# The gate of an RWKV-7 layer: computed per unit of the recurrence, or for half the sequence at a time and kept in DRAM

## The chip, the cores and the metric

The kernel runs on one core of a Trainium2 chip. The metric is device time in microseconds, one launch, median of the runs shown. Engines: PE (TensorE, matrix products), DVE (VectorE), ACT (ScalarE), POOL (GpSimd) and SP (SyncE, which here only issues DMAs). Each engine works through its instructions in the order in which they were written for it, and waits at an instruction until its operands are there.

## The reference, cut to what matters

One sequence of 1024 tokens, width 1024, float32. Two layers: an RWKV-7 time mixing with an MLP, then an attention layer with an MLP. The change lies in the RWKV-7 layer:

```
xg = h + (token_shift(h) - h) * mu[5]
g = sigmoid(xg @ g1) @ g2              # g1: 1024 x 160, g2: 160 x 1024, g: 1024 x 1024
...                                    # r, w, k, v, a in like manner; wkv7_scan gives y
y = groupnorm(y) * ln_w + ln_b + bonus
x = x + (1 + gt1) * ((y * g) @ wo)
x = x + (1 + gt2) * mlp(...)           # 1024 -> 4096 -> 1024, squared ReLU
```

The sigmoid's 160 outputs per token are the LoRA values. The gate g is their product with g2.

## The kernel before, in words

Activations lie with 128 channels on the partitions and tokens along the row: a matrix of 1024 channels is 8 tiles (`KT`), a half of the sequence is 512 tokens (`HT`).

**Large products.** `mm3` makes a product of float32 accuracy from three fp32r products: both operands are split into a high part (rounded to fp32r) and a low part (the rest), and high by high (line 124), low activation by high weight (126) and high activation by low weight (128) are summed. `load_w` fetches a weight tile of 128 x 1024 into `wraw` (115), ACT rounds it to `wh` (116), POOL subtracts to get `wl` (117). `wraw`, `wh` and `wl` have two buffers each (`NW = (2, 2)`), which every stream of weights shares. `proj` walks over 8 output tiles with one such weight each: 24 products for one half, 48 where both halves share a weight. It is a generator, and yields after each of the 8 steps.

**Small products** (the scan's, the LoRA's, the norm's) take float32 operands as they are; such a product appears as two PE instructions in the trace.

**The recurrence** runs in 16 units (`units`): 8 pairs of channel tiles by four quarters of 256 tokens, in this order: first half of the sequence for all pairs, then the second. Each unit has an `early` and a `late` part, which prepare it, a serial `chain` with priority, and afterwards a `gate`, run beside the next unit. At each stop of the chain, `step` takes so many steps of the others: `NA` (2.2 in units 0 to 6), `NC` and `NB` for the stream beside. That stream (`m0`, from `beside` in `run`) first finishes the projections (`dense`: v for the first half, then the second half's `lora_wa`, k, v, r streams and `lora_g`), waits until the first half's gates are done, and then goes on with the output projection `wo` and the MLP of the first half. After the units come 20 more steps of it (`ND`), then `wo` for the second half, and so on; `m1` is the second half's MLP. Later `phase_kv` makes the keys, values and forget gate logits that both halves of the attention layer use, with `proj` over both halves and the weights of K and V in turn; the forget gate's own weight (128 x 8 x 16) stands among them.

**The gate before.** `lora_g` makes the LoRA values for a half. 128 of them go to DRAM (`gad`), the last 32 to partitions 96 to 127 of `zt` in SBUF. `gate` norms the unit's y, fetches `ga` (128 x 256) and for each of two channel tiles a piece of g2, makes the gate with two float32 products (943, 944) into PSUM, and DVE multiplies (946):

```
PE.matmul(out=ps[:, c], lhsT=g2[:, 0], rhs=ga, start=True, stop=False)
PE.matmul(out=ps[:, c], lhsT=g2[96:128, 1], rhs=self.zt[96:128, ts], start=False, stop=True)
...
V.tensor_tensor(out=y, in0=y, in1=ps, op=ALU.mult)
```

**Who sets the order.** The code is written as one program; when it is built, a scheduler lays each engine's instructions in an order by its own estimate of times, within the dependences and priorities. A change in one place therefore reorders others, also far behind it.

Of the kernel before, what the change touches and what calls it, by code (L numbers as in the profile page):

```python
# [15 lines left out]
F32 = mybir.dt.float32  # L16
F32R = mybir.dt.float32r
BF16 = mybir.dt.bfloat16
AF = mybir.ActivationFunctionType
ALU = mybir.AluOpType  # L20
# [3 lines left out]
T = 1024  # L24
HT = 512
D = 1024
KT = 8
# [48 lines left out]
class K:  # L76
# [171 lines left out]
    def run(self, stop=99):  # L248
        tc, nc, ap = self.tc, self.nc, self.ap
        V, S = nc.vector, nc.scalar  # L250
        with ExitStack() as es:
# [45 lines left out]
            self.T16d = dt("T16d", [2 * KT, 2, 64, 256])  # L297
            self.gad = dt("gad", [128, T])

# [9 lines left out]
            zp = self.pool(er, "zp")  # L309
            self.zt = zp.tile([128, T], F32, name="zt")  # L310
            self.sv = zp.tile([128, KT, HD], F32, name="sv")
# [109 lines left out]
    NS = 1.5  # L421
    NA = 2.2
    NW = (2, 2)
# [22 lines left out]
    def phase_rwkv(self, es):  # L446
# [85 lines left out]

        def dense():
            yield from v
            yield from self.lora_wa(h, 1, lw, al)
            for i in (1, 2, 0):
                yield from self.stream(h, 1, i, xj, ev, al)
            yield from self.lora_g(h, 1, lw)

# [30 lines left out]
    def lora_g(self, h, j, lw):  # L570

        nc, S = self.nc, self.nc.scalar
        s = slice(j * HT, (j + 1) * HT)
        ps = [self.bank() for _ in range(2)]
        for k in range(KT):
            w = lw(("g1",), k)
            xg = self.mix(h[j][k], self.shift(h[j][k]), 5, k)
            for p, o, n in ((ps[0], 0, 128), (ps[1][96:128], 128, 32)):
                nc.tensor.matmul(out=p, lhsT=w[:, o:o + n], rhs=xg, start=k == 0, stop=k == KT - 1)
                yield  # L580
        g = self.t()
        for a, p in ((g, ps[0]), (self.zt[96:128, s], ps[1][96:128])):
            S.activation(out=a, in_=p, func=AF.Tanh, scale=0.5)
            nc.gpsimd.tensor_scalar(out=a, in0=a, scalar1=0.5, scalar2=0.5, op0=ALU.mult, op1=ALU.add)
        nc.sync.dma_start(out=self.gad[:, s], in_=g)

# [86 lines left out]
    def phase_wkv(self, es, rest, done):  # L673
# [18 lines left out]
        def lng(n, shape, bufs=2):  # L692
            return pool["s"].tile(shape, F32, name=n, tag=n, bufs=bufs)
# [228 lines left out]
        def gate(u, w):  # L922

            j, p, ts = where(u)
            y, bv, rs = w["y"], self.t(), self.t()
            ga = lng("ga", [128, 256], 1)
            nc.sync.dma_start(out=ga, in_=self.gad[:, ts])
            nc.sync.dma_start(out=two(bv), in_=pair(self.bvd, p, ts))
# [5 lines left out]
            S.activation(out=rs, in_=rs, func=AF.Exp, scale=-0.5)  # L934
            ps = self.small()
            for q in range(2):
                c = slice(q * 256, (q + 1) * 256)
                g2 = lng("g2", [128, 2, 128], 1)
                nc.sync.dma_start(out=g2[:, 0], in_=ap["g2"][p + q][0:128])
                nc.sync.dma_start(out=g2[96:128, 1], in_=ap["g2"][p + q][128:160])  # L940
                V.scalar_tensor_tensor(out=y[:, c], in0=y[:, c], scalar=self.col("lnw", p + q), in1=rs[:, c], op0=ALU.mult, op1=ALU.mult)
                V.scalar_tensor_tensor(out=y[:, c], in0=y[:, c], scalar=self.col("lnb", p + q), in1=bv[:, c], op0=ALU.add, op1=ALU.add)
                PE.matmul(out=ps[:, c], lhsT=g2[:, 0], rhs=ga, start=True, stop=False)
                PE.matmul(out=ps[:, c], lhsT=g2[96:128, 1], rhs=self.zt[96:128, ts], start=False, stop=True)
                yield
            V.tensor_tensor(out=y, in0=y, in1=ps, op=ALU.mult)
            nc.sync.dma_start(out=pair(self.yd, p, ts), in_=two(y))
# [522 lines left out]
```

## Time and profile before

| | |
|---|---|
| median of 3 runs | 3394.84 us (3390.83 to 3399.28) |
| the profiled execution | 3394.05 us, its span 3392.1 us |
| PE busy | 3214.4 us (95%) |
| DVE, ACT, POOL busy | 1943.0 (57%), 1432.8 (42%), 1358.7 (40%) |
| mean granted TensorE clock | 0.970 |

The span is the time from the first to the last instruction. A busy time is the time in which an engine works on some instruction; PE's products overlap, so a product's place in the row is best read as the distance from its start to the next one's start. The granted clock has two levels, full speed (2.4 GHz) and half of it (1.2 GHz); a figure between is a mean over a stretch. The units lie between about 243 and 1320 us.

### The profile page before, as it was taken

What the parts mean: (1) busy time and instruction counts of PE and PEld (TensorE: products, weight loads), DVE (VectorE), ACT (ScalarE), POOL (GpSimd) and SP (SyncE); (2) the same over time, 40 slices, a digit from 0 to 9 for tenths busy, and PEclk for the clock granted to TensorE, in tenths of its full rate; (3) what the DMA queues carried; (4) which work ended last, traced back from release to release, by engine and by line L of the source; (5) the groups of instructions that cost most, each with busy time, mean ns of one, the idle gap of its engine ahead of it and who ended that gap; (6) DMA issues with size and microseconds to landing.
All of it is one profiled execution on the core that took longest, in us unless ns stands there. A gap on an engine that the chain in (4) does not pass through costs nothing.

```text
span 3392.1 us, 50350 instructions
## 1 busy us (share of the span) xinstructions
PE 3214.4 (95%) x19108; PEld 2438.4 (72%) x19108; DVE 1943.0 (57%) x3239; ACT 1432.8 (42%) x2284; POOL 1358.7 (40%) x868
## 2 busy tenths in 40 slices
PE   4898999999999999899999999999999999999997
PEld 2456666666777776678887777777778888778886
DVE  7496765766556534167786433555566666454344
ACT  3642236523433223242233556667555544332323
POOL 3364432333333233354444432444423333454444
PEclk7899999899999999899999999999999999999999
DMA  7374344355333223236752233666544443232222
GB/s 276 98 234 151 95 128 135 116 152 150 88 102 102 85 76 125 68 111 224 229 187 88 85 131 119 207 203 182 177 128 136 144 134 100 88 111 95 98 98 83
DMA packets 294065, 452.90 MB, mean 134 GB/s; under 512 B 114720, under 2 KB 170432, under 8 KB 293824
## 3 DMA queue, kind: packets, MB, share of 16 engines
q1 hardware_dynamic: 293824, 449.68, 42.3%
q8 instruction: 152, 2.49, 0.3%
q14 instruction: 89, 0.73, 0.1%
HBM read 371.25 MB, written 78.32 MB: 133 GB/s over the span
## 4 chain that ended last, share of the span: by engine, by line
PE 50%; DVE 4%; ACT 2%; DMA 1%; issue 1%; POOL 1%; SPq 0%; DVEq 0%; ACTq 0%; POOLq 0%
PE pj L124 8%; PE pj L128 7%; PE pj L126 7%; PE pk L128 7%; PE pk L124 7%; PE pk L126 7%; PE pt L1328 2%; PE po L1313 1%; PE po L1314 1%; PE ps L1285 1%; PE ps L1286 1%; DVE t L239 1%; DVE hl L241 1%; DVE x L1016 1%; DVE modacc L185 0%
## 5 line engine op out<-in xcount | busy, mean ns | idle before, releaser
L117 POOL TENSOR_TENSOR wl<-wraw,wh 128x1024 fp32r<-128x1024 f32 x385 | 947.7, 2462 | 1231.7 <-ACT wh L116 1162.6
L116 ACT CAST wh<-wraw 128x1024 fp32r<-128x1024 f32 x385 | 402.6, 1046 | 822.0 <-PE pk L126 359.2
L124 PE MATMUL pj<-hh,wh 128*128 128x512 f32 x1120 | 448.6, 408 | 7.4 <-DVE sq L1090 2.7
L128 PE MATMUL pj<-hh,wl 128*128 128x512 f32 x1120 | 445.1, 403 | 5.5 <-POOL wl L117 5.5
L126 PE MATMUL pj<-hl,wh 128*128 128x512 f32 x1120 | 443.2, 401 | 0.0
L1016 DVE SCALAR_TENSOR_TENSOR x<-pj,G,x 128x512 f32<-128x512 f32 x304 | 225.8, 747 | 164.3 <-PE pj L128 162.2
L128 PE MATMUL pk<-hh,wl 128*128 128x512 f32 x688 | 272.1, 402 | 8.6 <-POOL wl L117 8.6
L124 PE MATMUL pk<-hh,wh 128*128 128x512 f32 x688 | 270.2, 398 | 8.9 <-ACT wh L116 7.8
L126 PE MATMUL pk<-hl,wh 128*128 128x512 f32 x688 | 267.3, 395 | 0.0
L124 PEld LDWEIGHTS pj<-hh,wh 128*128 128x128 f32 x1120 | 210.9, 189 | 61.9 <-issue 4.5
L1016 DVE SCALAR_TENSOR_TENSOR x<-pk,G,x 128x512 f32<-128x512 f32 x240 | 176.2, 746 | 135.7 <-PE pk L128 135.2
L128 PEld LDWEIGHTS pj<-hh,wl 128*128 128x128 f32 x1120 | 210.6, 188 | 58.9 <-POOL wl L117 7.7
L126 PEld LDWEIGHTS pj<-hl,wh 128*128 128x128 f32 x1120 | 211.1, 189 | 48.1 <-issue 2.4
L124 PE MATMUL pj<-mh,wh 128*128 128x512 f32 x564 | 236.9, 421 | 6.0 <-DVE mr L1046 3.0
L126 PE MATMUL pj<-ml,wh 128*128 128x512 f32 x564 | 224.3, 398 | 0.0
L128 PE MATMUL pj<-mh,wl 128*128 128x512 f32 x564 | 219.4, 399 | 2.4 <-POOL wl L117 2.4
L124 PE MATMUL pk<-mh,wh 128*128 128x512 f32 x460 | 182.1, 398 | 8.9 <-DVE mr L1046 5.4
L166 ACT CAST mh<-mr 128x512 fp32r<-128x512 f32 x128 | 79.5, 621 | 250.6 <-PE pj L128 109.1
L126 PE MATMUL pk<-ml,wh 128*128 128x512 f32 x460 | 181.7, 395 | 0.0
L185 DVE SCALAR_TENSOR_TENSOR modacc<-modw,cact,modacc 128x1024 f32<-128x1024 f32 x98 | 155.1, 1583 | 31.0 <-DMA modw<-in_modw_dram 22.5
L128 PE MATMUL pk<-mh,wl 128*128 128x512 f32 x460 | 166.6, 397 | 0.0
L124 PEld LDWEIGHTS pk<-hh,wh 128*128 128x128 f32 x688 | 130.7, 190 | 42.8 <-ACT wh L116 11.6
(334 smaller groups left out, 6493.2 us busy)
## 6 DMA issues: line engine op xcount, KB each, us to landing
wraw<-in_up_dram SPq DMA_DIRECT2D x128, 512.0 KB
wraw<-in_down_dram SPq DMA_DIRECT2D x128, 512.0 KB
modw<-in_modw_dram SPq DMA_DIRECT2D x96, 512.0 KB
wraw<-in_wqg_dram SPq DMA_DIRECT2D x32, 512.0 KB
wraw<-in_wk_dram SPq DMA_DIRECT2D x24, 512.0 KB
wraw<-in_wv_dram SPq DMA_DIRECT2D x24, 512.0 KB
x<-in_xT_dram SPq DMA_DIRECT2D x32, 256.0 KB
wraw<-in_wr_dram SPq DMA_DIRECT2D x16, 512.0 KB
```

Of the source, the lines that this page charges most:

```text
L116: nc.scalar.copy(out=wh, in_=raw)
L117: self.weng.tensor_tensor(out=wl, in0=raw, in1=wh.bitcast(F32), op=ALU.subtract)
L124: mm(out=p, lhsT=wh, rhs=hh[k], start=first, stop=False)
L126: mm(out=p, lhsT=wh, rhs=hl[k], start=False, stop=False)
L128: mm(out=p, lhsT=wl, rhs=hh[k], start=False, stop=last)
L166: self.nc.scalar.copy(out=out_h, in_=src)
L185: nc.vector.scalar_tensor_tensor(out=acc, in0=w, scalar=ck, in1=acc, op0=ALU.mult, op1=ALU.add)
L239: nc.vector.scalar_tensor_tensor(out=t, in0=x[k], scalar=A[:, k:k + 1], in1=rs, op0=ALU.mult, op1=ALU.mult)
L241: nc.vector.scalar_tensor_tensor(out=hl[k], in0=t, scalar=sh[:, k:k + 1], in1=hh[k].bitcast(F32), op0=ALU.add, op1=ALU.subtract)
L1016: self.nc.vector.scalar_tensor_tensor(out=x[j][m], in0=ps, scalar=gain[:, m:m + 1], in1=x[j][m], op0=ALU.mult, op1=ALU.add)
L1285: PE.matmul(out=o[:, 0:r], lhsT=qs[:, q], rhs=kh[:, i * n:i * n + r], start=True, stop=False)
L1328: PE.transpose(out=pt[:, i * 256 + b * 128:i * 256 + (b + 1) * 128], in_=Ps[b][:, (k + i) * 128:(k + i + 1) * 128], identity=ident)
```

## The change

A new generator `gates(j, ev)` makes the gates of a whole half: it reads the LoRA values of the half from DRAM (`gad` has 160 rows now), splits them, loads g2 as one weight tile by `load_w`, and a second weight tile `wr` that holds g2's last 32 rows three times: high part, high part and low part. For each of 8 channel tiles it makes three products over the first 128 LoRA values and one over the 96 stacked rows, all fp32r of 512 columns; ACT copies the result out and a DMA writes it to `gd`. `dense` runs `gates(0)` first and `gates(1)` last, and takes the second half's `lora_g` beside its last stream. `gate` only fetches its 128 x 512 piece of `gd`; its multiplication is on POOL. `NA` goes from 2.2 to 2.5.

```diff
-            self.gad = dt("gad", [128, T])
+            self.gad = dt("gad", [160, T])
+            self.gd = dt("gd", [KT, 128, T])
...
-    NA = 2.2
+    NA = 2.5
...
         def dense():
+            yield from self.gates(0, ev)
             yield from v
             yield from self.lora_wa(h, 1, lw, al)
-            for i in (1, 2, 0):
+            for i in (1, 2):
                 yield from self.stream(h, 1, i, xj, ev, al)
-            yield from self.lora_g(h, 1, lw)
+            yield from self.both(self.lora_g(h, 1, lw), self.stream(h, 1, 0, xj, ev, al), 2)
+            yield from self.gates(1, ev)
...
+    def gates(self, j, ev):
+        nc, S, V = self.nc, self.nc.scalar, self.nc.vector
+        s = slice(j * HT, (j + 1) * HT)
+        f = lambda n, d=F32R, b=1: ev.tile([128, HT], d, name=n, tag=n, bufs=b)
+        gh, gl, gr = f("e2"), f("e3"), f("e1", F32R, 2)
+        g, r = self.t(), self.t()
+        nc.sync.dma_start(out=g, in_=self.gad[0:128, s])
+        self.split(gh, gl, g)
+        nc.sync.dma_start(out=r[0:32], in_=self.gad[128:160, s])
+        S.copy(out=gr[0:32], in_=r[0:32])
+        S.copy(out=gr[64:96], in_=r[0:32])
+        V.tensor_tensor(out=gr[32:64], in0=r[0:32], in1=gr[0:32].bitcast(F32), op=ALU.subtract)
+        wh, wl = self.load_w(self.ap["g2"][:, 0:128].rearrange("m k n -> k m n"))
+        raw, wr = (self.wp.tile([128, KT, 128], d, name=n, tag=n, bufs=b) for n, d, b in (("wraw", F32, self.NW[0]), ("wh", F32R, self.NW[1])))
+        for i in range(3):
+            nc.sync.dma_start(out=raw[i * 32:(i + 1) * 32], in_=self.ap["g2"][:, 128:160].rearrange("m k n -> k m n"))
+        S.copy(out=wr[0:96], in_=raw[0:96])
+        self.weng.tensor_tensor(out=wr[64:96], in0=raw[64:96], in1=wr[64:96].bitcast(F32), op=ALU.subtract)
+        for m in range(KT):
+            p = self.bank()
+            self.mm3([p], wh[:, m], wl[:, m], [(j, [gh], [gl])], 0, True, False)
+            nc.tensor.matmul(out=p, lhsT=wr[0:96, m], rhs=gr[0:96], start=False, stop=True)
+            yield
+            o = f("e0", F32, 2)
+            S.copy(out=o, in_=p)
+            nc.sync.dma_start(out=self.gd[m][:, s], in_=o)
...
-            ga = lng("ga", [128, 256], 1)
-            nc.sync.dma_start(out=ga, in_=self.gad[:, ts])
+            g = lng("g", [128, W], 1)
+            nc.sync.dma_start(out=two(g), in_=pair(self.gd, p, ts))
...
-                g2 = lng("g2", [128, 2, 128], 1)
-                nc.sync.dma_start(out=g2[:, 0], in_=ap["g2"][p + q][0:128])
-                nc.sync.dma_start(out=g2[96:128, 1], in_=ap["g2"][p + q][128:160])
...
-                PE.matmul(out=ps[:, c], lhsT=g2[:, 0], rhs=ga, start=True, stop=False)
-                PE.matmul(out=ps[:, c], lhsT=g2[96:128, 1], rhs=self.zt[96:128, ts], start=False, stop=True)
-                yield
-            V.tensor_tensor(out=y, in0=y, in1=ps, op=ALU.mult)
+            yield
+            G.tensor_tensor(out=y, in0=y, in1=g, op=ALU.mult)
```

The change moves instructions in three places that matter below. The first is PE where the units have ended and `wo` for the second half begins. `wh_12536` (before) and `wh_12543` (changed) are the high part of the first half's last `down` weight, `hh` and `wh_12557` and so on belong to `wo`. Before:

```order
L128 MATMUL pj_12549<-mh_12189,wl_12537 128x512
L124 MATMUL pk_12568<-hh_12406,wh_12557 128x512
...
L128 MATMUL pk_12568<-hh_12448,wl_12558 128x512
L124 MATMUL pk_12569<-hh_12406,wh_12563 128x512
L126 MATMUL pk_12569<-hl_12407,wh_12563 128x512
...
L124 MATMUL pk_12786<-hh_12406,wh_12781 128x512
L126 MATMUL pk_12786<-hl_12407,wh_12781 128x512
L124 MATMUL pk_12839<-mh_12144,wh_12536 128x512
```

Changed:

```order
L128 MATMUL pj_12564<-mh_12200,wl_12544 128x512
L124 MATMUL pj_12572<-mh_12151,wh_12543 128x512
...
L128 MATMUL pj_12572<-mh_12200,wl_12544 128x512
L124 MATMUL pk_12591<-hh_12439,wh_12580 128x512
...
L128 MATMUL pk_12591<-hh_12481,wl_12581 128x512
L124 MATMUL pk_12592<-hh_12439,wh_12586 128x512
L126 MATMUL pk_12592<-hl_12440,wh_12586 128x512
```

Before, half of the `down` weight's 24 products come ahead of all of `wo` and the other half after its eighth weight has begun; now all 24 come ahead of `wo`.

The second place is PE in `phase_kv`, behind the forget gate's weight (`16x512`). Before:

```order
L124 MATMUL pj_16864<-hh_15962,wh_16859 16x512
...
L128 MATMUL pk_16809<-hh_16495,wl_16804 128x512
L1135 MATMUL pms_16924<-cs_60,sq_16922 128x128 x4
L124 MATMUL pk_16958<-hh_15962,wh_16953 128x512
...
L128 MATMUL pk_16959<-hh_16495,wl_16954 128x512
L124 MATMUL pk_17048<-hh_15962,wh_17043 128x512
```

Changed:

```order
L128 MATMUL pk_16872<-hh_16502,wl_16867 16x512
L1106 MATMUL pmt_16782<-sq_16780,blk_m_68 128x512
L1161 MATMUL pms_16931<-cs_60,sq_16929 128x128 x4
L124 MATMUL pk_17055<-hh_15969,wh_17050 128x512
...
L128 MATMUL pk_17056<-hh_16502,wl_17051 128x512
L1106 MATMUL pms_17017<-sq_17015,blk_m_68 128x512
L124 MATMUL pk_17152<-hh_15969,wh_17147 128x512
```

Before, the weights come in the order in which they were loaded (16803, 16953, 17043, 17140); now V's 17050 and K's 17147 follow each other while K's 16960, loaded earlier, is begun in between and ends after 17050 and during 17147.

The third place is POOL around a unit's gate (unit 3): `y` is the unit's output, `sp` an operand of the chain, `wl` a weight's low part. In the kernel before, the multiplication was on DVE and POOL had no such row. Changed:

```order
L899 TENSOR_TENSOR sp_4794<-st_4787,pc_3593 128x128
L117 TENSOR_TENSOR wl_5093<-wraw_5091,wh_5092 128x1024
L972 TENSOR_TENSOR y_4723<-y_4723,g_4749 128x512
L899 TENSOR_TENSOR sp_5013<-st_5006,pc_3593 128x128
L117 TENSOR_TENSOR wl_5272<-wraw_5270,wh_5271 128x1024
```

The new multiplication stands between the low parts of two weights, ahead of the chain's next `sp`.

## Rows read from the trace of the kernel before

**Rows 1.** The page's head and parts 1 and 2 (40 equal slices).

```profile
span 3392.1 us, 50350 instructions
PE 3214.4 (95%) x19108; PEld 2438.4 (72%) x19108; DVE 1943.0 (57%) x3239; ACT 1432.8 (42%) x2284; POOL 1358.7 (40%) x868
PE   4898999999999999899999999999999999999997
```

**Rows 2.** Busy time by stretch; columns as in the first line.

```profile
core 0: us, PE busy (x) PEld busy (x) DVE busy (x) ACT busy (x) POOL busy (x), PEclk, DMA share, GB/s
243.00:1320.00 1077.00, 1040.24 (x9177) 732.04 (x9176) 640.38 (x1375) 389.50 (x603) 382.85 (x298) 0.97 0.40 117
1320.00:1342.00 22.00, 21.84 (x95) 17.36 (x94) 12.89 (x17) 9.11 (x14) 7.93 (x4) 1.00 0.61 223
1342.00:1405.00 63.00, 47.30 (x149) 33.55 (x147) 5.15 (x7) 10.45 (x13) 19.07 (x10) 0.84 0.16 50
1840.00:2140.00 300.00, 294.13 (x1280) 227.06 (x1279) 126.62 (x192) 165.91 (x228) 105.91 (x58) 0.99 0.35 118
```

**Rows 3.** Instruction groups, 240 to 1320 us, shapes apart: busy, mean; idle before.

```profile
L943 PE MATMUL pms<-ga,g 128*128 128x256 f32 x64 | 21.2, 413 | 0.0
L944 PE MATMUL pms<-zt,g 32*128 32x256 f32 x64 | 22.2, 426 | 0.0
...
L757 POOL TENSOR_TENSOR bk<-bk,sg 128x512 f32<-128x512 f32 x15 | 19.3, 1284 | 26.6 <-DVE sg L756 26.6
...
L946 DVE TENSOR_TENSOR y<-y,pms 128x512 f32<-128x512 f32 x16 | 11.0, 685 | 6.9 <-PE pms L944 6.9
```

**Rows 4.** PE in order of time: start, length, line, operands, count; unit 15.

```profile
1313.67 0.39 PE L126 MATMUL pj<-ml,wh 128*128 128x512 f32 x1
1313.90 0.40 PE L128 MATMUL pj<-mh,wl 128*128 128x512 f32 x1
1314.16 0.70 PE L943 MATMUL pms<-ga,g 128*128 128x256 f32 x2
1314.79 0.69 PE L944 MATMUL pms<-zt,g 32*128 32x256 f32 x2
1315.41 0.50 PE L124 MATMUL pj<-mh,wh 128*128 128x512 f32 x1
```

**Rows 5.** All engines in order of time, `wo` for the second half.

```profile
1342.45 1.04 ACT L116 CAST wh<-wraw 128x1024 fp32r<-128x1024 f32 x1 [7.67 <-PE pk L126]
1343.55 0.50 PE L124 MATMUL pk<-hh,wh 128*128 128x512 f32 x1 [0.95 <-ACT wh L116]
1343.57 2.35 POOL L117 TENSOR_TENSOR wl<-wraw,wh 128x1024 fp32r<-128x1024 f32 x1 [6.32 <-ACT wh L116]
1345.98 0.50 PE L128 MATMUL pk<-hh,wl 128*128 128x512 f32 x1 [1.70 <-POOL wl L117]
...
1348.38 0.63 PE L124 MATMUL pk<-hh,wh 128*128 128x512 f32 x1
1348.80 0.63 PE L126 MATMUL pk<-hl,wh 128*128 128x512 f32 x1
...
1353.86 0.50 PE L124 MATMUL pk<-hh,wh 128*128 128x512 f32 x1 [0.94 <-ACT wh L116]
...
1405.27 0.50 PE L124 MATMUL pk<-hh,wh 128*128 128x512 f32 x1 [0.95 <-ACT wh L116]
```

**Rows 6.** Who waited for whom, 1340 to 1406 us: total, times, longest.

```profile
ACT wh L116 <- PE pk L126: 42.4, 5, 8.7
PE pk L128 <- POOL wl L117: 6.8, 4, 1.7
```

**Rows 7.** The same, 240 to 1320 us.

```profile
POOL sp L867 <- DVE st L910: 113.0, 29, 9.7
PE pj L126 <- DVE xl L167: 13.4, 8, 4.5
```

**Rows 8.** PE's waits, 1840 to 2140 us.

```profile
PE pk L124 <- ACT wh L116: 2.0, 1, 2.0
```

More of the change, by code (lines that the diff above doesn't have):

```diff
@@ L309, in run @@
             zp = self.pool(er, "zp")
-            self.zt = zp.tile([128, T], F32, name="zt")
+            self.zt = zp.tile([65, T], F32, name="zt")
             self.sv = zp.tile([128, KT, HD], F32, name="sv")
@@ L577, in lora_g @@
             xg = self.mix(h[j][k], self.shift(h[j][k]), 5, k)
-            for p, o, n in ((ps[0], 0, 128), (ps[1][96:128], 128, 32)):
+            for p, o, n in ((ps[0], 0, 128), (ps[1][0:32], 128, 32)):
                 nc.tensor.matmul(out=p, lhsT=w[:, o:o + n], rhs=xg, start=k == 0, stop=k == KT - 1)
                 yield
[L581 to L584, printed above, removed]
@@ L585, in lora_g @@
-        nc.sync.dma_start(out=self.gad[:, s], in_=g)
+        for p, o, n in ((ps[0], 0, 128), (ps[1], 128, 32)):
+            g = self.t()
+            S.activation(out=g[0:n], in_=p[0:n], func=AF.Tanh, scale=0.5)
+            nc.gpsimd.tensor_scalar(out=g[0:n], in0=g[0:n], scalar1=0.5, scalar2=0.5, op0=ALU.mult, op1=ALU.add)
+            nc.sync.dma_start(out=self.gad[o:o + n, s], in_=g[0:n])
+    def gates(self, j, ev):
[24 more added lines that the diff above has]
+            nc.sync.dma_start(out=self.gd[m][:, s], in_=o)
@@ L934, in gate @@
             S.activation(out=rs, in_=rs, func=AF.Exp, scale=-0.5)
-            ps = self.small()
             for q in range(2):
                 c = slice(q * 256, (q + 1) * 256)
-                g2 = lng("g2", [128, 2, 128], 1)
-                nc.sync.dma_start(out=g2[:, 0], in_=ap["g2"][p + q][0:128])
-                nc.sync.dma_start(out=g2[96:128, 1], in_=ap["g2"][p + q][128:160])
                 V.scalar_tensor_tensor(out=y[:, c], in0=y[:, c], scalar=self.col("lnw", p + q), in1=rs[:, c], op0=ALU.mult, op1=ALU.mult)
                 V.scalar_tensor_tensor(out=y[:, c], in0=y[:, c], scalar=self.col("lnb", p + q), in1=bv[:, c], op0=ALU.add, op1=ALU.add)
-                PE.matmul(out=ps[:, c], lhsT=g2[:, 0], rhs=ga, start=True, stop=False)
-                PE.matmul(out=ps[:, c], lhsT=g2[96:128, 1], rhs=self.zt[96:128, ts], start=False, stop=True)
-                yield
-            V.tensor_tensor(out=y, in0=y, in1=ps, op=ALU.mult)
+            yield
+            G.tensor_tensor(out=y, in0=y, in1=g, op=ALU.mult)
             nc.sync.dma_start(out=pair(self.yd, p, ts), in_=two(y))
```

## The prediction

> **What bounds the kernel.** The page's head and parts 1 and 2 come first: PE is busy 95% of the span, and nearly every slice shows 9 [rows 1]. So a change counts by the PE time that it takes away and by the PE idle time that it makes or ends. The stretches come next [rows 2]. In the units PE is busy 1040.24 of 1077 us; 37 us are idle, and the largest named wait there is 13.4 us for `xl` in the streams [rows 7]. Right behind the units PE is full, and then, from 1342 to 1405, it is busy only 47.30 of 63 us, at a mean granted clock of 0.84, with no other engine near full. In `phase_kv` and around it (1840 to 2140) only 6 us of 300 are idle. The change touches the units by its own work, and the other two stretches by the order alone.
>
> **The change part by part.**
>
> *Products taken away.* The two float32 products stand in the trace as 64 instructions each [rows 3], two to a product [rows 4], so 32 + 32 products. Their starts lie 0.63 us apart, and the next line begins 0.62 us after the second [rows 4]: 0.625 us each, 64 x 0.625 = 40.0 us of PE.
>
> *Products added.* Two halves by 8 tiles by 4 = 64 fp32r products of 512 columns. Neighbours of that kind start 0.23 us apart [rows 4]: 14.7 us. Net 25.3 us less PE work. The products' lengths, 413 and 426 ns by instruction [rows 3], overlap and are no price; they would give 43 us instead of 40.
>
> The Trainium skill (FP8 and Floating Point Precision, "TensorE Precision Notes") says that a true float32 product goes through the array in four passes. Four passes of 256 columns would be twice an fp32r product of 512 as the rows show it, 0.46 us, and the net 14.7 us instead of 25.3; the rows show 0.625, so the trace has something on top of the passes here, and it decides.
>
> *The stretch from 1342 to 1405.* This is `wo` for the second half: 24 products to a weight. The cast of each weight waits until PE has done the last product that reads the weight before (5 such waits in one bank, two more in the other) [rows 6]; then PE waits 0.95 us for the cast and 1.70 us for the low part [rows 5]. A cast that waits for the previous weight's end means that only one buffer of `wh` serves the stream. The order shown with the change tells why: the paused `down` weight keeps the other until it is finished behind the eighth `wo` weight. From 1343.55 to 1405.27 PE begins six weights [rows 5]: 10.29 us each, against 24 x 0.23 = 5.5 us of products. Some of the 4.8 us more is the half clock after the waits, where starts lie 0.42 us apart [rows 5]. In the changed order the `down` weight is finished ahead of `wo`, because the stream beside has made a different number of steps by then (16 more in `gates`, 0.3 more a stop in units 0 to 6). Then the next weight is cast during the one at work: 1.04 us of ACT and 2.35 us of POOL [rows 5] inside 5.5 us. I take the whole loss as gone: 6 x 4.8 + 0.95 = 29.7 us. What is late next is the weights' transfer, 512 KB in 5.5 us or 95 GB/s; the stretch before it, with other work, moved 223 GB/s [rows 2].
>
> *`phase_kv`.* Here the same mechanism runs the other way. Before, two weights take turns. In the changed order a held weight leaves one buffer for five handovers (to 17050, 17147, 17351, 17727 and 17903, each 0 to 2 products of a weight's and one to five small ones behind the end of the one before); the forget gate's small weight is a sixth, but short. Cast and low part together are 3.4 us [rows 5]; the small products and the first `wh` products cover about 1 us, which leaves 2.4 us each. The ends: nothing, if the evacuations which stand there hold PE anyway, and 4.8 us as in `wo`. The nearest row, a single wait for a cast in this stretch, has 2.0 us [rows 8]. I take 5 x 2.4 = 12 us, between 0 and 24.
>
> *The weights of `gates`.* They take both buffers, so the stream's next weight cannot be cast until the last gate product but one or so: one uncovered handover in and one out, for each half. For the first half the order has few products to cover them, for the second the chain's small products stand there. I take 4 us, between 0 and 10 (two at 4.8); below nothing, if the extra dense work fills PE's idle time in the units, at most some 5 of the 37 us.
>
> *Beside the path.* The multiplication goes from DVE (685 ns) to POOL; a POOL product of that shape takes 1284 ns [rows 3], so 16 x 1.28 = 20.5 us more on an engine that is busy 383 of 1077 us [rows 2]: at no cost while POOL has slack, 20.5 us if each stood in PE's way. ACT gets 16 copies of PSUM and six casts, DVE a few subtractions, both under 60% busy; SP issues about 30 DMAs fewer. The copies share their two `e0` buffers with transfers to DRAM; this is inside the 0 to 10 above. The wait that `gate` newly has, for `g` from DRAM, stands on a DMA issued a unit ahead; behind it on POOL stand `sp` and a weight's low part (see the fourth rival).
>
> *Sum.* From the profiled execution, 3394.05 us (its span 3392.1 and 2 us around it, 0.8 below the median): - 25.3 - 29.7 + 12 + 4 = 3355 us; beside the median 3356.
>
> **The rivals.**
>
> 1. `wo` keeps its period: the 10.29 us are then a transfer's or POOL's, not a buffer's. For it: that stretch moves just 50 GB/s [rows 2], so slow transfers are not excluded by it. Against: the cast waits for PE, not for a DMA [rows 5, 6]. Time: 3356 + 29.7 = 3386.
>
> 2. The units are held by the chain and not by PE, so that fewer products there only turn into idle time. For it: `sp` waits 113.0 us in total for the chain's state [rows 7]. Against: PE is idle in only 37 of 1077 us [rows 2]. Time: 3356 + 25.3 = 3381.
>
> 3. The handovers in `phase_kv` and at `gates` are covered by waits that are there anyway. Time: 3356 - 16 = 3340. For it: the mean wait for weights in that stretch is small before, although one handover there is bare too. Against: a weight's preparation needs 3.4 us, and the order has less between.
>
> 4. Slower: POOL's order. Each multiplication stands ahead of the chain's next `sp` and a weight's low part, and waits for the norm of y; in a serial queue the chain waits with it. Price: 1.28 us of work plus a wait of up to that for a state, 9.7 us at the longest [rows 7]. With 16 units it decides from (3394 - 3356 + 10) / 16 = 3.0 us a unit; at 4.5 us the time is 3356 + 72 = 3428. For it: POOL now stands between the chain and the gate. Against: POOL idles two thirds of the units, and the gate runs a unit behind the chain.
>
> The Trainium skill (GPSIMD Engine Reference, "Engine selection") advises against this: an elementwise product of two tiles belongs on VectorE, and is about twice as slow on GPSIMD. By that rule, the trace agrees in the size, 1284 against 685 ns [rows 3]; whether it costs time is the fourth rival's question.
>
> **How the numbers follow.** A measurement of this kernel can tell about 0.3% from no change, 10 us: faster is below 3384.7, slower above 3405.0. Chances: the forecast 0.60 (its own range 3343 to 3372), rival 1 0.12, rival 2 0.09, rival 3 0.13, rival 4 0.06. Faster: 0.60 + 0.13 from the third, 0.07 of the second and 0.05 of the first = 0.85. Within 0.3%: the rest of the first two, 0.09. Slower: 0.06. The range: at the low end both gains whole and nothing added, with the 5 us of filled idle time, 3394 - 55 - 5 = 3334; at the high end both unknown costs at their upper bounds, 24 + 10 instead of 16, and half the products' gain lost to the chain, 3356 + 18 + 13 = 3387, which takes in rivals 1 and 2.
>
> **What would show it.** In the changed profile: no product with operand `ga`, and 64 products more on `mm3`'s lines and the new line 613; PE's busy time some 25 us lower in the units, which end about 20 us earlier; in `wo` for the second half no waits for the cast, starts of weights 5.5 to 6 us apart and a granted clock near 1.00; in `phase_kv` PE waiting for `wh` and `wl` at five places, 2 to 3 us each. Wrong would be: `wo` at 10 us a weight again (rival 1), units as long as before with more PE idle (rival 2), or chain products that wait for `sp` behind the new multiplication (rival 4).

## The result, and the profile after

The changed kernel takes 3425.32 us (median of 4 runs, 3422.31 to 3426.93) where the kernel before takes 3395.44 (4 runs, 3390.83 to 3399.28): a ratio of 1.0088, interval 1.0070 to 1.0105. It is slower by 30 us; the forecast was 3356 us, range 3334 to 3387. The profiled execution took 3426.93 us, its span is 3425.1.

The head and parts 1 and 2 of the page, which answer to [rows 1]:

```profile
span 3425.1 us, 50190 instructions
PE 3215.2 (94%) x19044; PEld 2450.3 (72%) x19044; DVE 1964.8 (57%) x3227; ACT 1449.3 (42%) x2308; POOL 1388.3 (41%) x888
PE   4798999999999999999999999899999999999998
PEclk7897998799999999999999999999999999999999
```

PE has 64 instructions fewer and is as busy as before: 3215.2 us against 3214.4 [rows 1]. An instruction at the lower clock counts as busy for longer (large products start 0.42 us apart there, 0.23 at the full clock [rows 5, 4]), and the granted clock is 7 or 8 tenths in five of the first eight slices.

Three landmarks are in both traces: the end of the last unit (its copy of y), the first copy of a square out of PSUM (L1132, now L1158), and the first attention product (L1285, now L1311). Between them:

| stretch | before | after | difference | forecast |
|---|---|---|---|---|
| 190 us to the last unit's end | 1113.6 | 1146.6 | +33.0 | -21 (-25.3 + 4) |
| to the first square (`wo`, feed-forward) | 632.5 | 598.0 | -34.5 | -29.7 |
| to the first attention product (`phase_kv`) | 198.0 | 221.3 | +23.3 | +12 |
| to the last attention product | 707.3 | 718.5 | +11.2 | 0 |
| to the end of the span | 550.6 | 550.7 | 0 | 0 |

The landmarks do not cut the work quite alike: the changed kernel's `phase_kv` row holds 893 PE instructions, the kernel before 861, and the rows on either side of it hold 22 and 19 fewer. Some us of the `wo` row's gain and of the `phase_kv` row's loss are such work.

Busy time by stretch, after (columns: stretch, length, busy time and instructions of PE, PEld, DVE, ACT and POOL, granted clock, DMA share, GB/s): the units, the place in `wo` that answers to the third stretch of [rows 2], and `phase_kv`.

```profile
190.00:1336.60 1146.60, 1080.12 (x9275) 764.98 (x9273) 695.26 (x1413) 413.99 (x641) 442.45 (x330) 0.94 0.42 126
1366.00:1410.00 44.00, 43.98 (x192) 35.73 (x191) 10.94 (x16) 12.25 (x15) 25.86 (x13) 1.00 0.30 98
1934.00:2157.00 223.00, 208.47 (x900) 155.79 (x900) 82.66 (x130) 123.34 (x174) 63.56 (x38) 0.98 0.36 121
```

The same view of the kernel before, 190 us to its last unit's end:

```profile
190.00:1303.60 1113.60, 1075.03 (x9328) 751.26 (x9326) 678.57 (x1424) 397.02 (x616) 411.86 (x312) 0.97 0.41 123
```

In `wo` PE is full at clock 1.00: that gain came as forecast. The units lost nearly as much as it gave. There PE is idle for 1146.6 - 1080.1 = 66.5 us, where it was 38.6. The trace's clock records show 143.4 us of the stretch at 1.2 GHz, where it was 61.4; half of that, 71.7 and 30.7 us, is what the lower level took (a few us less, since PE was idle in 12 and 7 us of it). What is left, the work at the full clock, fell from 1044.3 to 1008.4. So some 36 us of work went, and 28 us of idle time and about 40 us of clock came.

All of the loss lies ahead of the end of unit 10, which came at 974.5 us instead of 927.1. The five units behind it, in which PE is idle for only 3 us of 362, got shorter, from 376.5 to 362.1 us, about as much as five units' products at the forecast's price (12.5 us).

PE's waits in units 1 to 10, after (378 to 975 us: who waits for whom, total us, times, longest):

```profile
PE pq L938 <- DVE uv L931: 10.8, 4, 5.0
PE pq L907 <- DVE st L942: 3.3, 5, 1.2
PE pq L938 <- DVE st L942: 3.0, 3, 1.8
PE pq L907 <- DVE sv L942: 2.9, 3, 2.1
PE pq L907 <- DVE xs L924: 2.7, 2, 2.5
PE py L947 <- ACT uv L930: 2.6, 3, 1.2
```

These are the chain's own products, which wait for the chain's own values: 25 us in the six rows. Before, the same units (378 to 928 us) show:

```profile
...
PE pq L875 <- DVE st L910: 3.9, 2, 2.9
PE pq L875 <- DVE st L908: 1.6, 1, 1.6
PE py L915 <- ACT uv L898: 1.4, 2, 0.8
PE pq L906 <- DVE st L910: 1.1, 1, 1.1
PE pq L906 <- DVE uv L899: 1.0, 2, 0.6
```

That is 9 us. Over the whole stretch PE's waits grew by 24 us. Those of the chain's products grew by 15, waits of other products for ACT by 11 and for transfers by 5; others fell. The chain has become the largest thing that PE waits for, but it is not the only one.

### The profile page after: what moved, and what is told of

It is laid out like the page before. It is cut to its first block, busy times and chain, and to the rows that moved or that the text cites. A ratio compares the mean times of both kernels' runs of the same rounds, so it can differ in the third digit from the quotient of the medians.

```text
span 3425.1 us, 50190 instructions
## 1 busy us (share of the span) xinstructions
PE 3215.2 (94%) x19044; PEld 2450.3 (72%) x19044; DVE 1964.8 (57%) x3227; ACT 1449.3 (42%) x2308; POOL 1388.3 (41%) x888
## 4 chain that ended last, share of the span: by engine, by line
PE 52%; DVE 5%; ACT 2%; DMA 2%; POOL 1%; issue 1%; SPq 0%; DVEq 0%; ACTq 0%; POOLq 0%
PE pj L124 8%; PE pj L128 8%; PE pj L126 8%; PE pk L128 7%; PE pk L124 7%; PE pk L126 7%; PE pt L1354 2%; PE po L1340 1%; PE po L1339 1%; DVE t L239 1%; PE ps L1311 1%; PE ps L1312 1%; DVE hl L241 1%; POOL wl L117 1%; DVE x L1042 0%
## 5 line engine op out<-in xcount | busy, mean ns | idle before, releaser
L128 PE MATMUL pk<-hh,wl 128*128 128x512 f32 (+1 forms) x704 | 270.6, 399 | 6.9 <-POOL wl L117 6.9
L124 PE MATMUL pk<-hh,wh 128*128 128x512 f32 (+1 forms) x704 | 269.5, 396 | 5.3 <-ACT wh L116 3.0
L126 PE MATMUL pk<-hl,wh 128*128 128x512 f32 (+1 forms) x704 | 268.3, 395 | 0.0
L128 PEld LDWEIGHTS pk<-hh,wl 128*128 128x128 f32 (+1 forms) x704 | 130.8, 187 | 42.6 <-POOL wl L117 11.1
```

The costliest lines, as they stand in the source:

```text
L124: mm(out=p, lhsT=wh, rhs=hh[k], start=first, stop=False)
L126: mm(out=p, lhsT=wh, rhs=hl[k], start=False, stop=False)
L128: mm(out=p, lhsT=wl, rhs=hh[k], start=False, stop=last)
```

## The experiments

Theories on the units' 33 us. **W**: products are work of a busy PE (the prediction). **F**: the chain's latency is a unit's floor, and work that is taken from under it turns into idle PE and half clock. **P**: POOL's new multiplication holds the chain. **D**: the rate of 2.5 dense instructions a stop. **M** and **G**: the gates' streams, by their place or by what they bring.

All runs at once: ratio to the kernel before with its interval; of the profiled execution the stretch from 190 us to the last unit's end, PE's idle time in it, and half its time at 1.2 GHz (us). The same units, instruction for instruction on PE, stand in the changed kernel and in e8_banks: 1146.6 and 1140.2 us. So a stretch alone tells no less than some 6 us.

| kernel | us | ratio, interval | units | idle | clock |
|---|---|---|---|---|---|
| before | 3395 to 3399 | 1 | 1113.6 | 38.6 | 30.7 |
| changed | 3425.3 | 1.0088 (1.0070-1.0105) | 1146.6 | 66.5 | 71.7 |
| e1_mult_dve | 3436.7 | 1.0108 (1.0088-1.0127) | 1160.3 | 73.6 | 81.9 |
| e2_na22 | 3418.1 | 1.0045 (1.0028-1.0061) | 1139.1 | 65.2 | 71.7 |
| e3_before_na25 | 3438.9 | 1.0113 (1.0096-1.0131) | 1149.3 | 58.3 | 46.1 |
| e4_before_nd24 | 3373.4 | 0.9917 (0.9897-0.9937) | 1114.3 | 39.3 | 30.7 |
| e5_gates0_early | 3420.8 | 1.0065 (1.0046-1.0085) | 1147.3 | 72.0 | 71.7 |
| e6_lorag_tail | 3418.9 | 1.0070 (1.0051-1.0088) | 1154.1 | 75.1 | 66.6 |
| e7_both_moves | 3427.0 | 1.0089 (1.0074-1.0104) | 1149.9 | 75.0 | 66.6 |
| e8_banks | 3399.0 | 1.0011 (1.0001-1.0020) | 1140.2 | 69.9 | 59.8 |
| e9_no_products | 3387.3 | 0.9969 (0.9954-0.9984) | 1105.0 | 58.6 | 44.4 |
| e10_gates_beside | 3428.6 | 1.0088 (1.0071-1.0105) | 1146.9 | 49.9 | 47.8 |
| e11_banks_na22 | 3392.3 | 0.9984 (0.9974-0.9993) | 1128.3 | 53.7 | 70.0 |
| e12_pe_only | 3401.6 | 1.0010 (0.9998-1.0022) | 1119.2 | 35.5 | 29.0 |
| e13_gates0_only | 3459.0 | 1.0169 (1.0147-1.0190) | 1151.1 | 50.3 | 56.3 |
| e14_gates1_only | 3436.5 | 1.0107 (1.0084-1.0130) | 1135.5 | 40.4 | 51.2 |
| e15_no_copies | 3412.9 | 1.0046 (1.0029-1.0063) | 1132.5 | 42.4 | 39.3 |
| e16_copies_only | 3426.6 | 1.0084 (1.0067-1.0101) | 1145.9 | 52.0 | 51.2 |
| e17_before_na21 | 3389.5 | 0.9979 (0.9966-0.9992) | 1104.8 | 43.1 | 23.9 |
| e18_na21_nd12 | 3363.4 | 0.9906 (0.9889-0.9922) | 1103.5 | 41.4 | 22.2 |

### First: the multiplication, the rate, and wo

**e1_mult_dve**, on the changed kernel:

```diff
-            G.tensor_tensor(out=y, in0=y, in1=g, op=ALU.mult)
+            V.tensor_tensor(out=y, in0=y, in1=g, op=ALU.mult)
```

> The changed kernel with the gate's last multiplication (L972) on VectorE again; everything else as changed. Theory P (POOL's order and POOL's work beside VectorE delay the chain, rival 4 of the prediction): the units' stretch loses most of its 68 us of idle PE, and the time falls from 3425 to 3400 or below. Theory D (the number of dense instructions put beside each stop of the chain, raised from 2.2 to 2.5, is what starves or delays the chain): no more than 5 us of change, 3420 to 3428. Theory G (the gates' own stream in front of the dense work disturbs the first units): the same as under D. The chain's scaled state (POOL, L899) should be late less often under P alone.

11 us slower than the changed kernel: P is refuted, and so is the fourth rival's mechanism. Its sign is absent too: VectorE, which reads `sp`, waited for it in neither kernel, and all that waited for the new multiplication was one cast, for 0.6 us. POOL's wait for the chain's state (240 us to the last unit's end) in e1, and in the changed kernel:

```profile
POOL sp L899 <- DVE st L942: 147.4, 32, 17.3
```

```profile
POOL sp L899 <- DVE st L942: 109.0, 30, 15.0
```

With 681 ns a unit more on VectorE, the state itself comes later, and VectorE makes the state. POOL was the better place.

**e2_na22** (changed kernel) and **e3_before_na25** (kernel before), each with the other's rate:

```diff
-    NA = 2.5
+    NA = 2.2
```

> The changed kernel with 2.2 dense instructions beside each stop of the chain, as before the change, instead of 2.5. Theory D: the units' stretch runs as before or better, the wo stage keeps its gain, and the time is 3365 to 3400. Theories P and G: no gain, or a longer time since the dense work, with the gates' instructions in it, lasts over more units: 3420 to 3440.

> The kernel before with 2.5 dense instructions beside each stop of the chain instead of 2.2, and nothing else. Theory D: slower by 15 to 35 us (3410 to 3430). Theories P and G: within 8 us of the kernel before (3387 to 3403).

The rate costs 7 us in the changed kernel and 40 us in the kernel before, more than D expected. In e3 the dense stream ends at 773 us instead of 785, but `wo`'s first half may begin only behind the eighth gate (L328, `while self.ngated < KT: yield`). Until then no stream stands beside the chain; the first result of that half comes at 831.5 us, before at 809.6. The hole, in e3:

```profile
773.00:805.00 32.00, 27.74 (x314) 20.10 (x313) 15.61 (x36) 11.67 (x20) 6.69 (x12) 0.80 0.61 170
```

Idle time and clock cost some 10 us in it; that the rest of the 40 follows from it is argued. In the changed kernel the gates' stream lasts to 822 us, and that gate's multiplication comes at 811, so there is no such hole; that the rate costs less there for this reason is argued too. D explains 7 of the 33 us, not more.

**e4_before_nd24**, on the kernel before:

```diff
-    ND = (20, 40)
+    ND = (24, 40)
```

> The kernel before, with its paused weight of the wo stage's neighbour finished: 24 instead of 20 of the down projection's pieces are done ahead of wo's second half, so that no half-used weight keeps one of the two wh buffers while wo runs. If the period of 10.29 us per weight in that stage comes from the held buffer: the stage's period falls to about 5.5 us, and the time to about 3366 (3360 to 3375). If wo keeps its period for another reason (rival 1): 3390 to 3398.

The same stretch as the third of [rows 2], in e4:

```profile
1342.00:1405.00 63.00, 63.00 (x273) 51.01 (x272) 12.23 (x16) 17.57 (x22) 34.98 (x18) 1.00 0.28 92
```

63.00 of 63 us at clock 1.00, and 26 us less in all; from the last unit's end to the first square it is 603.1 us, 29.4 less than before. The mechanism that the prediction read out of [rows 5, 6] is shown, and it needs nothing of the change but that the half-used weight goes.

### Second: places, and phase_kv

**e5_gates0_early** and **e6_lorag_tail**, on the changed kernel with NA = 2.2 (e5 also with ND = (12, 40)), and **e7_both_moves**, both together:

```diff
 (e5)    def dense():
-            yield from self.gates(0, ev)
             yield from v
 (e5)    def rest():
...
+            yield from self.gates(0, ev)
             self.drain(m)
 (e6)    def dense():
-            for i in (1, 2):
+            for i in (1, 2, 0):
                 yield from self.stream(h, 1, i, xj, ev, al)
-            yield from self.both(self.lora_g(h, 1, lw), self.stream(h, 1, 0, xj, ev, al), 2)
+            yield from self.lora_g(h, 1, lw)
```

> The changed kernel with 2.2 dense instructions beside a stop, as in e2_na22, and with the first half's gates made before the units begin (at the end of what is drained ahead of them) instead of at the head of the dense stream; 12 instead of 20 of the down projection's pieces ahead of wo, so that no half-used weight stands there in this order either. Theory M (the gates at the head push the second half's LoRA operands, which POOL and VectorE mix, out of unit 0 and beside the chain of unit 1): those products run within unit 0 again (they ended at 366 us before and at 393 us after), units 1 to 5 lose at most half of e2's 23.6 us of idle PE, and the time is 3375 to 3403. Theory F (the chain's own latency is the floor of a unit; PE work that is taken away only turns idle): the time stays at e2's 3418 within 8 us.

> The changed kernel with 2.2 dense instructions beside a stop, as in e2_na22, and with the second half's gate LoRA after its three streams again, as before the change, instead of between the pieces of the last stream. Theory M, its second half (the LoRA's 16 operand mixes, spread over units 5 and 6, hold VectorE and POOL against the chain): units 5 and 6 lose their 38 us of idle and half clock down to the 17 of before, and the time is 3395 to 3410. Theory F: 3418 within 8 us.

> Both moves of e5_gates0_early and e6_lorag_tail together: the products are gone and the gates are made, but no operand mixing stands beside another unit than before the change. Theory M: the sum of the two gains, 3355 to 3385, and faster than the kernel before. Theory F: 3410 to 3426.

All three stay within 9 us of e2, e7 1 us above the range that F gave it; M is refuted. In e5 unit 1 takes 48 us instead of e2's 66, but the part up to unit 0's end, with the gates in it, 171 instead of 134. The loss only moved.

**e8_banks**, on the changed kernel:

```diff
+            self.nbank += 2
             self.phase_kv(x, rs, kv, hp1, q, ev)
```

> The changed kernel, with two PSUM banks of the rotation skipped ahead of phase_kv, so that its position among the six is that of the kernel before; nothing else. If the five bare handovers of a weight in phase_kv come from the rotation that 16 more bank calls have shifted: the stretch from the first vector of the square's copies to the first attention product falls from 221 us to 198 to 205, and the time to 3403 to 3412. If phase_kv is longer for another reason (what reaches it from the units): 3420 to 3428.

26 us faster than the changed kernel, more than expected. PE's waits in `phase_kv`, changed kernel (1934 to 2157 us), then e8 (1936 to 2136 us):

```profile
PE pmt L1161 <- DVE sq L209: 6.1, 2, 5.5
PE pk L128 <- POOL wl L117: 5.1, 5, 1.3
PE pk L124 <- ACT wh L116: 1.6, 1, 1.6
```

```profile
PE pms L1162 <- ACT sq L1159: 3.0, 1, 3.0
PE pk L128 <- POOL wl L117: 0.4, 1, 0.4
```

The kernel before (1936 to 2135 us):

```profile
PE pms L1135 <- ACT sq L1132: 3.0, 1, 3.0
```

The stretch falls from 221.3 to 199.5 us and attention from 718.5 to 709.6, while `wo` rises from 598.0 to 605.7: some of the work that had crossed the landmark is back. So the shifted rotation of PSUM banks, and the order that comes with it, made the loss in `phase_kv`. For attention this is less sure: over all runs it takes 711 to 719 us with the rotation of the changed kernel and 705 to 712 with that of the kernel before. e13 and e14, with 8 bank calls more in place of 16, have a third rotation, and 211 and 210 us there with 720 and 722 us of attention.

### Third: the change taken apart in the units

**e9_no_products**, on the kernel before; what it leaves out is the gate's value:

```diff
-            ga = lng("ga", [128, 256], 1)
-            nc.sync.dma_start(out=ga, in_=self.gad[:, ts])
...
-            ps = self.small()
+            self.nsmall += 1
...
-                PE.matmul(out=ps[:, c], lhsT=g2[:, 0], rhs=ga, start=True, stop=False)
-                PE.matmul(out=ps[:, c], lhsT=g2[96:128, 1], rhs=self.zt[96:128, ts], start=False, stop=True)
...
-            V.tensor_tensor(out=y, in0=y, in1=ps, op=ALU.mult)
+            V.tensor_tensor(out=y, in0=y, in1=bv, op=ALU.mult)
```

> The kernel before without the 64 gate products in the units and the loads of their operands (the gate then multiplies by another tile that is there; what is left out is the gate's value); no gates' stream, nothing else moved. Theory W (the products are work of a busy PE, as the prediction has it): 64 x 0.625 us = 40 us less in the stretch from 190 us to the last unit's end, 1114 to 1074 us, and a time of 3356 to 3362. Theory F (the chain is a unit's floor in the first eleven units; work that is taken away there turns into idle PE, and the idle PE into half clock): only the five last units, which ran without a gap, get shorter, by 2.5 us each, and the time is 3378 to 3390.

10 us faster instead of 40: F. Unit 10 ends at 926.7 us, where it ended at 927.1 with the products, so eleven units gave nothing; the five behind it are 8.2 us shorter, where F had 12.5. The stretch, in e9:

```profile
190.00:1295.00 1105.00, 1046.39 (x9202) 741.69 (x9202) 693.75 (x1422) 394.04 (x615) 406.60 (x311) 0.96 0.41 121
```

Work at the full clock fell by 42 us (1044.3 to 1105.0 - 58.6 - 44.4 = 1002.1), which is the prediction's price of 40 for the products. But the idle time grew by 20 and the clock's loss by 14. PE's waits for the chain in units 1 to 10 (378 to 927 us) grew with nothing added:

```profile
PE pq L906 <- DVE uv L899: 5.9, 4, 2.3
PE pq L906 <- DVE st L910: 4.2, 4, 3.4
...
PE py L915 <- ACT uv L898: 2.7, 4, 1.2
...
PE pq L875 <- DVE xs L892: 2.0, 4, 0.9
```

**e10_gates_beside**, on the kernel before: the streams are made and not read.

```diff
         def dense():
+            yield from self.gates(0, ev)
             yield from v
...
             yield from self.lora_g(h, 1, lw)
+            yield from self.gates(1, ev)
```

> The kernel before with the two gates' streams made as well, at the changed kernel's two places of the dense stream, but not read: the units keep their products, and 2.2 instructions beside a stop. In this order wo holds no half-used weight (a gain of 26 as e4_before_nd24 measured it) and phase_kv has the shifted rotation (a loss of about 26 as e8_banks measured it), so that these two cancel. Theory W or F, the streams cost their own 14.7 us of PE work and nothing else: 3405 to 3415. Theory G (the streams' weights, splits and copies hold up the units around them): 3420 or more, with the units 0 to 2 and 8 to 10 longer than before.

The time is in G's range, and the stretch grew by 33.3 us. With e9's -8.6 that makes +24.7; e2, which has both at the same rate, has +25.5. By the medians it is 31.4 - 9.9 = 21.5, and e2 has 18.7. So the totals add up, but the places do not: at the end of unit 10 the two together make +22.6 where e2 has +34.2, and in the five units behind it +2.1 where e2 has -8.7. The close agreement of the totals is in part luck.

**e11_banks_na22** is e8 with NA = 2.2.

> The changed kernel with both edits that have helped it: two banks skipped ahead of phase_kv (e8_banks, -26) and 2.2 instructions beside a stop (e2_na22, -7). If the two are independent: 3390 to 3395, level with the kernel before. If what the second gave was given in phase_kv and not in the units: 3396 to 3402.

As expected of independent gains, and level with the kernel before.

**e12_pe_only**, e10 with this in place of all loads, splits, copies and writes; the gates' values are left out:

```diff
+        gr = ev.tile([128, HT], F32R, name="e1", tag="e1", bufs=2)
+        S.copy(out=gr, in_=self.hx[j][0][:, 1:HT + 1])
+        for m in range(KT):
+            p = self.bank()
+            for i in range(4):
+                nc.tensor.matmul(out=p, lhsT=gr[:, 0:128], rhs=gr, start=i == 0, stop=i == 3)
+            yield
```

> As e10_gates_beside, but of each gates' stream only its 32 products are left, on one resident tile in place of their operands: no weights are loaded or split, nothing is copied out of PSUM or written to DRAM (the gates' values are left out; the units still make their own). If the place is the cost (the dense work behind is later against the units): the units' stretch stays near e10's 1147 us (1138 to 1150) and the time near 3428 (3418 to 3430). If the weights, splits and copies are the cost: the stretch falls to 1120 to 1131 and the time to 3402 to 3412.

**e13_gates0_only** and **e14_gates1_only** are e10 with the first or the second of its two added lines alone.

> As e10_gates_beside, with the first half's gates' stream alone (at the head of the dense work). In this order wo keeps its half-used weight, and phase_kv its old rotation, so that the time tells the units' stretch alone. If the head of the dense stream is the costly place (theory M): 3415 to 3425. If the later place is: 3400 to 3408. If both share it: 3409 to 3415.

> As e10_gates_beside, with the second half's gates' stream alone (at the end of the dense work, where wo's first half waits behind it). wo and phase_kv as in e13. If the head is the costly place: 3400 to 3408. If this place is (wo's first half and the feed-forward work start later and are left over after the units): 3415 to 3425. If both share it: 3409 to 3415.

e12: the 64 products at their places cost 6 us of the stretch, so place is not the cost. PE is no less full than before; the rest of the 33 us is what the streams bring. e13 and e14 are misses: the time was to tell the units alone, and the bank rotation spoiled that (above), and in the units one stream costs 37.5 or 21.9 us where both cost 33.3. Which of the two is the costly one stays open; their costs don't add. Since each of these kernels also has an order of its own from the scheduler, some of each difference may be the order's, in e10, e15 and e16 too: a rate of 2.1 in place of 2.2 (e17, below) moves the stretch by 9 us.

**e15_no_copies** is e10 without, **e16_copies_only** e12 with, these lines in `gates`:

```diff
             o = f("e0", F32, 2)
             S.copy(out=o, in_=p)
             nc.sync.dma_start(out=self.gd[m][:, s], in_=o)
```

> As e10_gates_beside, but nothing is copied out of PSUM or written to DRAM by the gates' streams (their values are left out; the units still make their own); their weights and LoRA values are loaded and split, and the same products run. If the loads and splits are the cost: the units' stretch stays at 1138 to 1150 us and the time at 3420 to 3430. If the copies and writes are: 1119 to 1128 us and 3400 to 3410. If neither alone, but the order that comes of all of it: between, 3410 to 3420.

> As e12_pe_only, with the copies out of PSUM and the writes to DRAM put back (16 copies of 128x512 on ACT, 16 DMAs); no weights or LoRA values are loaded or split, and what is written is not the gates. If the loads and splits are the cost: as e12, 3398 to 3408. If the copies and writes are: 3420 to 3430. If neither alone: 3408 to 3420.

In the units: e12 1119.2, e15 1132.5 (loads and splits, +13), e16 1145.9 (copies and writes, +27), e10 1146.9 (both, +28); by the times +11, +25 and +27. The copies and writes are the larger part, though 16 copies of 0.585 us are 9.4 us of ACT. e15 came out between its two cases, as its third had it (neither alone), e16 as the second. Where the time goes, and what PE waits for (end of unit 10; length of the five units behind it; sums of PE's waits from 190 us to the last unit's end; us):

| kernel | unit 10 ends | units 11 to 15 | chain's products | others, for ACT | others, for transfers |
|---|---|---|---|---|---|
| before | 927.1 | 376.5 | 10.4 | 3.1 | 0 |
| e9_no_products | 926.7 | 368.3 | 18.2 | 9.4 | 0 |
| e12_pe_only | 926.6 | 382.5 | 11.1 | 3.3 | 0 |
| e15_no_copies | 944.5 | 378.0 | 12.3 | 4.4 | 4.1 |
| e16_copies_only | 949.2 | 386.7 | 14.8 | 15.9 | 3.5 |
| e10_gates_beside | 950.1 | 386.8 | 11.0 | 14.2 | 7.4 |
| changed | 974.5 | 362.1 | 25.7 | 14.5 | 5.1 |

This speaks for two mechanisms, of which only one is the chain's. Without the products (e9) PE waits more for the chain, and some more for ACT; with the streams (e10) it waits no more for the chain than before, but more for ACT and for transfers. The changed kernel has both.

Waits in e16, ACT's from 190 to 1340 us and PE's from 378 to 950:

```profile
ACT e L604 <- DMA gd<-e: 26.3, 6, 8.6
```

```profile
PE pj L601 <- ACT e L604: 7.4, 2, 4.6
```

L604 is the copy. Six times it stood at the head of ACT's queue, 8.6 us at the longest, until a transfer to DRAM gave one of the two `e0` buffers back, and twice PE then waited for the copy. ACT's row in e10, and both in the changed kernel (190 to 1340 us):

```profile
ACT e L617 <- DMA gd<-e: 12.6, 5, 6.2
```

```profile
ACT e L616 <- DMA gd<-e: 7.6, 3, 4.3
PE pj L124 <- ACT e L616: 1.6, 2, 1.2
```

There the wait is half of e16's and less than a third of it, while e10 loses as much as e16. So this wait is not the whole cost. What in the copies and writes makes the rest (ACT's time, the transfers, the order) stays open, and deeper buffering was not tried.

**e17_before_na21** (kernel before, NA = 2.1) and **e18_na21_nd12** (the same with ND = (12, 40)):

> The kernel before with 2.1 dense instructions beside a stop instead of 2.2. If the units' time follows the amount of dense work smoothly: within 6 us of the kernel before (3391 to 3403), since 0.3 more cost e3 39 us only by ending the dense stream before wo may start. If the order by itself moves the units' idle PE as much as the streams did: 10 us or more away, either side.

> The kernel before with 2.1 dense instructions beside a stop (as e17) and 12 instead of 20 of the down projection's pieces ahead of wo's second half, the number that in this order leaves no half-used weight there (as 24 did in e4). If the two gains are independent: 3397 - 26 - 7 = 3364 (3358 to 3370), the fastest kernel of this study. If e17's 7 us was chance of the order or comes back in wo: 3369 to 3378.

e17 gains 7 us, just outside its expectation for a smooth course and short of the 10 us that it had for the order by itself. e18 is the sum of e4 and e17 as expected, 34 us under the kernel before and 62 under the changed one, without any of the change.

## Why the prediction was wrong

- **The step that failed is the sum's two terms for the units, -25.3 and +4; +33 was measured.** It counted a change by the PE time that it takes away. The price of the products was right (42 against 40), their worth was not: 9 to 10 of it came out (e9). For the products the second rival, with a chance of 0.09, had the mechanism, in units 0 to 10; in the five units in which PE is full the step nearly held (8 of 12.5 us). Its 3381 us is not what came, since the streams, which it had at the forecast's price, cost more. What spoke against it there, "PE is idle in only 37 of 1077 us", was misread: a small idle time says that the fill just covers the chain's latency, not that the chain has slack beneath it.
- **The gates' streams** were priced at 14.7 us for their products and 4 us, 0 to 10, for all else, copies included; they cost 33 us of the units (e10), 6 for the products at their places (e12) and 28 for loads, splits, copies and writes. The rows to read were ACT's: it is under 40% busy, but it works in order, and PE's waits for ACT are what grew with the streams (3 to 14 us). That the copies act by holding up the values and casts behind them is argued; the buffers that the prediction named explain at most a part.
- **The rate** had no cost in the sum, only a possible gain of 5 us from extra dense work, although its order was read for `wo`: 7 us here, 40 alone.
- **`wo`** was right in mechanism and nearly in size: forecast -29.7; -34.5 in the changed kernel's stretch, which has handed some work on, -29.4 in e4's, and -26 by e4's times.
- **`phase_kv`** was right in sign. The five handovers show, at 5.1 + 1.6 us of waits for the weights, less than the 12 forecast; but the order that the shifted bank rotation makes costs 23 us there, and 11 stand in attention, which the forecast had at nothing. The term was mis-sized: 12, bound 24, measured 34 in the two stretches. Some of that is work handed on by `wo`; two skipped banks take back 26 us by the times (e8).
- **POOL's multiplication** cost less than it saved on VectorE. By the Trainium skill (GPSIMD Engine Reference, "Engine selection") such a product belongs on VectorE; the instruction is slower on POOL as it says (1300 against 681 ns), but here the run with it on VectorE is the slower one by 11 us, since VectorE carries the chain.
- **Luck:** the time lies near the fourth rival's 3428 us, but nothing of that rival's mechanism shows.

Sum: -8.6 for the products, +33.3 for the streams, +7.5 for the rate (0.8 left over), -34.5 for `wo`, +34.5 for `phase_kv` and attention: +33 in the two profiles, which is 3425.1 - 3392.1. The forecast's 3355 us for this execution missed by 72: 31 by the products, 15 by the streams, 8 by the rate and what is left over, 22 by `phase_kv` and attention, less 5 by `wo`.

## What to carry to other kernels

When dense work is laid beside a serial chain, price a removal by running the kernel without it, not by its instructions' time: as long as the fill just covers the chain's latency, less fill is idle time and a lower clock. Where the fill has PE busy throughout, as in the last five units here, the price by instructions holds. An added stream is priced with its loads, copies and writes, not with its products alone (28 us against 6 here). And when one edit changes how often a buffer rotation is called, look at every later stage which that rotation serves, and try to realign it (here two skipped banks were worth 26 us).

## What the hardware showed beyond that

Idle time on PE came with time at the lower clock, but at no fixed price. In e9 20 us more of gaps came with 14 us more lost to the clock, in the changed kernel 28 us with 41, and in e8, with the changed kernel's PE order in the units, 31 us with 29. In e14 2 us of gaps more came with 20 us of clock. So the total of the gaps does not tell what the clock will cost.

Small VectorE products stretched while POOL ran a long two-input one. The changed kernel in order of time (start, length, engine, line):

```profile
422.72 4.65 POOL L117 TENSOR_TENSOR wl<-wraw,wh 128x1024 fp32r<-128x1024 f32 x2
...
422.82 2.28 DVE L805 TENSOR_TENSOR ti<-ti,tm 64x15 f32<-64x15 f32 x1
...
425.13 2.28 DVE L804 TENSOR_TENSOR tm<-lblk,ti 64x28 f32<-64x28 f32 x1
...
427.44 0.18 DVE L805 TENSOR_TENSOR ti<-ti,tm 64x28 f32<-64x28 f32 x1
...
428.34 0.29 DVE L931 COPY uv<-pq 64x128 f32<-64x128 f32 x1
...
428.68 0.48 PE L938 MATMUL pq<-uv,bkt 128*64 128x64 f32 x4 [5.00 <-DVE uv L931]
```

Two products of 0.2 us take 2.28 us each, as long as one of POOL's, and the chain's copy behind them makes PE wait 5.00 us. The Trainium skill (GPSIMD Engine Reference, "Key points") says that POOL shares its SBUF interfaces with VectorE, and that instructions of VectorE with two SBUF inputs are among those that contend; the trace agrees. It happened before the change too (22 of 480 such products took over 1 us, 36 after). It is not the cause of the loss: e12 has 35 of them and loses 6 us in the units, e14 has 21 and loses 22.
